# Strassen weight sums: three POOL adds per pair replaced by three more accumulating DMAs

## The chip, the core and the metric

The kernel runs on one core of a Trainium2 chip. The metric is the device time of one execution in microseconds. Engines: PE multiplies matrices, DVE, ACT and POOL work element by element, SP only issues transfers. Each engine takes its instructions in a fixed order and waits at the head of its queue.

## The reference

One inference step of a two-layer decoder: 512 prompt tokens and 64 sample tokens, width 1024, all in fp32.

```
h = RMSNorm(x)
P = h @ w_in                      # projections of four mixers, and gate logits G (4 x 1024 columns)
o_b = mixer_b(P_b)                # HGRN2, GLA, RWKV-7, RetNet, 256 wide each
x = x + (sum_b sigmoid(G_b) * (o_b @ w_branch[b])) @ w_out
g, u = split(RMSNorm(x) @ w_ffn_in)          # 2 x 2816 columns
x = x + (silu(g) * u) @ w_ffn_out
```

After the last layer `y = RMSNorm(x)`. The outputs are y for both groups and the mixers' states.

## The kernel before

Activations lie with channels on the partitions and the 576 tokens in the free dimension, in two halves of 288. An fp32 product is made of three fp16 matmuls: a value is split into a high part (ACT: scaled copy to fp16, L1692) and a low part (DVE: the value times 256 less the high part, L1693); then high x high, high x low and low x high are added in PSUM (L1718 to L1720).

Two places use Strassen's scheme in Winograd's form: the last two gate groups of each layer (`last_gates`, 8 pairs per layer) and most of the first feed-forward product (`ffn`, 19 pairs per layer, one for each 128 columns of g and of u). A pair takes two blocks of 128 output columns and the whole input depth of 1024, cut in two: four fp32 blocks of weights a11, a12, a21, a22, each 128 partitions x 512. Seven products (12 matmuls each) instead of eight use the blocks A11, A12, A22 and four sums of blocks: S1 = A21 + A22, S2 = S1 - A11, S3 = A11 - A21, S4 = A12 - S2. The sums of tokens (T4, tiles `st` and `mt`) are made once per layer.

`strassen_weights` makes the weights of one pair, as a generator in nine steps. In step 2 POOL issues a DMA that adds a22 to a21 where it lies (L1698). In steps 3 to 5 A11, A22 and A12 are split, and after each split POOL overwrites the block with a difference (L1696). In steps 6 to 9 the four sums are split. `strassen` makes the seven products of a pair; after each product it advances the generators: steps 6 to 9 of the present pair after products 1 to 4, steps 2 to 5 of the next pair after products 4 to 7. DVE then adds up products (su and sc, L1734). In the feed-forward stage sc goes through Silu on ACT (fsg, L1763), a product on DVE (fy, L1765) and a split (fa, L250); in the gates through Tanh, a product with the branch (gu, L1539) and an add on POOL (mg, L1540).

The written order is not the last word: a scheduler with its own costs sets the order of instructions on each engine. Weights are loaded by SP's queue into rings of a few buffers; the accumulating DMAs are on POOL's queue, where each waits for its operands before it is issued.

Of the kernel before, what the change touches and what calls it, by code (L numbers as in the profile page):

```python
# [16 lines left out]
ADD, SUB, MUL, MAX, MIN = ALU.add, ALU.subtract, ALU.mult, ALU.max, ALU.min  # L17
# [157 lines left out]
class Net:  # L175
# [14 lines left out]
    def t(self, ring, shape, name, dt=F32):  # L190

        assert int(np.prod(shape[1:])) * (2 if dt == F16 else 4) <= SIZE[ring], (shape, name)
        return self.rings[ring].tile(list(shape), dt, tag=ring, name=name)
# [51 lines left out]
    def split(self, out_hi, out_lo, src, scale=1.0):  # L245

        nc = self.nc
        nc.scalar.activation(out_hi, src, AF.Copy, scale=scale)
        if scale == 1.0:
            nc.vector.tensor_tensor(out_lo, src, out_hi, op=SUB)  # L250
        else:
            nc.vector.scalar_tensor_tensor(out_lo, src, scale, out_hi, op0=MUL, op1=SUB)
# [1410 lines left out]

    def strassen_tokens(self):

        nc = self.nc
        out = [self.t("gd", [128, 4, 2, HW], f"st{i}", F16) for i in range(4)]
        h0, h1 = slice(0, HW), slice(HW, T)  # L1670
        src = []
        for k in range(4):
            b11, b12, b21, b22 = (self.x[k + o][:, h] for o in (0, 4) for h in (h0, h1))
            for i, (dst, a, b) in enumerate(((b11, b12, b11), (b12, b22, b12), (b22, b22, b11), (b21, b21, b22))):
                nc.gpsimd.tensor_tensor(dst, a, b, op=SUB)
                src.append(((0, 2, 1, 3)[i], k, dst))
        yield out
        for i in (3, 1, 0, 2):
            for j, k, dst in src:
                if i == j:  # L1680
                    self.split(out[i][:, k, 0], out[i][:, k, 1], dst)
            yield out

    def strassen_weights(self, key, load, ring, **rings):

        nc = self.nc
        a11, a12, a21, a22 = load()
        w = self.sw[key] = {}

        def split(name, a):  # L1690
            hl = w[name] = self.t(rings.get(name, ring), [128, 2, 4, 128], "h" + name, F16)
            nc.scalar.activation(hl[:, 0], a, AF.Copy, scale=WS)  # L1692
            nc.vector.scalar_tensor_tensor(hl[:, 1], a, WS, hl[:, 0], op0=MUL, op1=SUB)  # L1693

        def add(dst, a, b, op):
            nc.gpsimd.tensor_tensor(dst, a, b, op=op)  # L1696
        yield
        nc.gpsimd.dma_start(out=a21, in_=a22, accum_op=ADD)  # L1698
        yield
        for name, a, op0, op1 in (("A11", a11, a21, a11), ("A22", a22, a22, a11), ("A12", a12, a12, a11)):  # L1700
            split(name, a)
            add(a, op0, op1, SUB)
            yield
        for name, a in (("S2", a11), ("S1", a21), ("S3", a22), ("S4", a12)):
            split(name, a)
            yield

    def strassen(self, w, t, prep, ps3, ring, then=None):


        nc = self.nc
        h0, h1 = slice(0, HW), slice(HW, T)

        def product(ring, a, rhs):
            ps = self.psum(ring, [128, HW], "fs" + a)
            for k in range(4):
                hi, lo = rhs(k)
                nc.tensor.matmul(ps, w[a][:, 0, k], hi, start=k == 0, stop=False)  # L1718
                nc.tensor.matmul(ps, w[a][:, 0, k], lo, start=False, stop=False)  # L1719
                nc.tensor.matmul(ps, w[a][:, 1, k], hi, start=False, stop=k == 3)  # L1720
                if k % 2:
                    yield
            next(prep, None)
            return ps

        def b(o, hs):
            return lambda k: (self.h[k + o][:, 0, hs], self.h[k + o][:, 1, hs])

        def tt(i):
            return lambda k: t(i, k)  # L1730

        def plus(a, p, name):
            o = self.t(ring if name[1] == "c" else "gt", [128, HW], name)
            nc.vector.tensor_tensor(o, a, p, op=ADD)  # L1734
            if then and name[1] == "c":
                then(o)
            return o
        p1 = self.t("gt", [128, HW], "sp1")
        nc.scalar.copy(p1, (yield from product("b", "A11", b(0, h0))))
        c11 = plus(p1, (yield from product("b", "A12", b(4, h0))), "sc11")  # L1740
        p4 = yield from product("g", "A22", tt(3))
        u2 = plus(p1, (yield from product("b", "S2", tt(1))), "su2")
        p5 = yield from product("g", "S1", tt(0))
        u4 = plus(u2, p5, "su4")
        u3 = plus(u2, (yield from product(ps3, "S3", tt(2))), "su3")
        c22 = plus(u3, p5, "sc22")
        c21 = plus(u3, p4, "sc21")
        c12 = plus(u4, (yield from product(ps3, "S4", b(4, h1))), "sc12")
        return c11, c12, c21, c22

    def ffn(self, l):
# [191 lines left out]
```

## Time and profile before

| | us |
|---|---|
| median of three runs (lowest, highest) | 2241.27 (2237.95, 2241.97) |
| the profiled execution | 2235.82 |
| its span in the trace | 2234.1 |
| PE busy in the span | 2047.3 (92%) |
| DVE busy | 1677.4 (75%) |
| ACT busy | 1070.6 (48%) |
| POOL busy | 652.0 (29%) |

An engine's share is a mean over stages with different limits: the feed-forward stage alone (784 to 988 us in layer 0) looks different. A busy matmul of 0.29 us overlaps the next ones. The first feed-forward product lies at 735 to 988 us (its first three column blocks without Strassen), the last gates at 530 to 690.

### The profile page before, as it was taken

Reading aid. Unit: us, or ns where it says so; the run is one execution under the profiler, and the core shown is the slowest. Engines: PE = TensorE matmul, PEld = TensorE weight load, DVE = VectorE, ACT = ScalarE, POOL = GpSimd, SP = SyncE. Lnnn points to the kernel's source line nnn. Section 1 sums busy time; section 2 is a strip of 40 time slices with the busy share of each in tenths; the row PEclk is TensorE's granted clock in tenths of the full one; section 3 lists DMA queues with packets and bytes.
Section 4 is the critical chain, followed back from the end, with each engine's and each line's share of the span. In section 5 each row is a group of like instructions: output and inputs, shape, how many; then the busy total and the mean of one; then the engine's idle time right before and its main releaser. Section 6 shows DMA issues by size and latency. Waiting matters only on the chain.

```text
span 2234.1 us, 42266 instructions
## 1 busy us (share of the span) xinstructions
PE 2047.3 (92%) x15754; PEld 1616.7 (72%) x15754; DVE 1677.4 (75%) x3719; ACT 1070.6 (48%) x2400; POOL 652.0 (29%) x850
## 2 busy tenths in 40 slices
PE   7988899898989999999998889889998988999998
PEld 5766676686767677777776667768776766777776
DVE  7889856868786899973488996686687768998531
ACT  6554545436454655442466344363554455554332
POOL 2212212245550544320011131222365415443000
PEclk9999999999999999999999999999999999999999
DMA  6312213333436244343421222142344443443431
GB/s 179 82 36 66 54 52 91 94 77 84 108 100 200 59 118 126 88 132 108 120 69 51 54 56 60 51 116 72 79 98 104 124 144 93 118 116 93 126 105 50
DMA packets 373497, 209.58 MB, mean 94 GB/s; under 512 B 59810, under 2 KB 360410, under 8 KB 373292
## 3 DMA queue, kind: packets, MB, share of 16 engines
q1 hardware_dynamic: 365516, 192.73, 31.1%
q0 software_dynamic: 7776, 14.16, 3.5%
q8 instruction: 124, 2.03, 0.4%
q14 instruction: 81, 0.66, 0.1%
HBM read 173.72 MB, written 16.59 MB: 85 GB/s over the span
## 4 chain that ended last, share of the span: by engine, by line
PE 47%; DVE 31%; ACT 8%; issue 7%; DMA 4%; POOL 3%; SPq 0%; DVEq 0%; ACTq 0%; POOLq 0%
PE pb L243 4%; PE pb L241 4%; PE pb L242 4%; PE xb L243 4%; PE xb L242 4%; PE xb L241 4%; DVE hA L1693 3%; DVE hS L1693 2%; DVE whl L229 2%; DVE sc L1734 2%; DVE fy L1765 2%; DVE qg L1111 2%; PE fsS L1720 2%; PE fsS L1718 2%; PE fsS L1719 2%
## 5 line engine op out<-in xcount | busy, mean ns | idle before, releaser
L241 PE MATMUL pb<-h,whl 128*128 128x288 f16 (+1 forms) x1504 | 439.9, 293 | 3.7 <-ACT h L463 2.2
L243 PE MATMUL pb<-h,whl 128*128 128x288 f16 (+1 forms) x1504 | 439.7, 293 | 2.7 <-DVE whl L229 2.7
L242 PE MATMUL pb<-h,whl 128*128 128x288 f16 (+1 forms) x1504 | 439.5, 292 | 0.6 <-DVE h L464 0.4
L229 DVE SCALAR_TENSOR_TENSOR whl<-raw,whl 128x512 f16<-128x512 f32 (+1 forms) x352 | 251.7, 725 | 132.0 <-ACT whl L228 130.3
L243 PEld LDWEIGHTS <-whl 128*128 128x128 f16 (+1 forms) x2784 | 277.3, 100 | 88.4 <-issue 11.0
L242 PEld LDWEIGHTS <-whl 128*128 128x128 f16 (+1 forms) x2784 | 276.7, 99 | 87.4 <-issue 11.0
L241 PEld LDWEIGHTS <-whl 128*128 128x128 f16 (+1 forms) x2784 | 279.0, 100 | 77.0 <-issue 3.6
L228 ACT ACTIVATE whl<-raw 128x512 f16<-128x512 f32 (+1 forms) x352 | 213.0, 616 | 167.4 <-PE pb L243 58.1
L243 PE MATMUL xb<-fa,whl 128*128 128x288 f16 x704 | 201.3, 286 | 0.0
L242 PE MATMUL xb<-fa,whl 128*128 128x288 f16 x704 | 201.3, 286 | 0.0
L241 PE MATMUL xb<-fa,whl 128*128 128x288 f16 x704 | 201.3, 286 | 0.0
L1718 PE MATMUL fsA<-h,hA 128*128 128x288 f16 x432 | 123.5, 286 | 14.4 <-DVE gu L1539 9.1
L1718 PE MATMUL fsS<-st,hS 128*128 128x288 f16 x456 | 131.1, 287 | 6.0 <-ACT hS L1692 6.0
L1720 PE MATMUL fsS<-st,hS 128*128 128x288 f16 x456 | 131.2, 288 | 0.9 <-DVE hS L1693 0.9
L1719 PE MATMUL fsS<-st,hS 128*128 128x288 f16 x456 | 131.1, 287 | 0.0
L1720 PE MATMUL fsA<-h,hA 128*128 128x288 f16 x432 | 123.6, 286 | 1.6 <-DVE hA L1693 1.6
L1719 PE MATMUL fsA<-h,hA 128*128 128x288 f16 x432 | 123.5, 286 | 0.0
L1696 POOL TENSOR_TENSOR raw<-raw 128x512 f32<-128x512 f32 x52 | 79.5, 1529 | 133.8 <-DVE hA L1693 129.7
L1718 PEld LDWEIGHTS <-hS 128*128 128x128 f16 x864 | 85.1, 99 | 35.5 <-ACT hS L1692 14.1
L1693 DVE SCALAR_TENSOR_TENSOR hA<-sraw,hA 128x512 f16<-128x512 f32 x110 | 101.5, 930 | 10.4 <-ACT hA L1692 9.7
L1696 POOL TENSOR_TENSOR sraw<-sraw 128x512 f32<-128x512 f32 x60 | 89.9, 1501 | 50.0 <-DVE hA L1693 45.5
L1720 PEld LDWEIGHTS <-hS 128*128 128x128 f16 x864 | 85.2, 99 | 24.6 <-DVE hS L1693 3.0
(487 smaller groups left out, 5271.1 us busy)
## 6 DMA issues: line engine op xcount, KB each, us to landing
raw<-in_w_in SPq DMA_DIRECT2D x208, 256.0 KB
sraw<-in_w_ffn_in SPq DMA_DIRECT2D x40, 512.0 KB
raw<-in_w_ffn_out SPq DMA_DIRECT2D x80, 256.0 KB
raw<-in_w_ffn_in SPq DMA_DIRECT2D x78, 256.0 KB
x<-xd SPq DMA_DIRECT2D x32, 288.0 KB
raw<-sraw POOLq DMA_DIRECT2D x34, 256.0 KB, 3.3
sraw<-in_w_in SPq DMA_DIRECT2D x32, 256.0 KB
raw<-in_w_out SPq DMA_DIRECT2D x32, 256.0 KB
```

The costliest lines, as they stand in the source:

```text
L228: nc.scalar.activation(hl[:, 0, :n], raw[:, :n], AF.Copy, scale=WS)
L229: nc.vector.scalar_tensor_tensor(hl[:, 1, :n], raw[:, :n], WS, hl[:, 0, :n], op0=MUL, op1=SUB)
L241: nc.tensor.matmul(ps, wh, hi, start=i == 0, stop=False)
L242: nc.tensor.matmul(ps, wh, lo, start=False, stop=False)
L243: nc.tensor.matmul(ps, wl, hi, start=False, stop=i == len(ks) - 1)
L1111: nc.vector.tensor_tensor(qo, qq, ee, op=MUL)
L1693: nc.vector.scalar_tensor_tensor(hl[:, 1], a, WS, hl[:, 0], op0=MUL, op1=SUB)
L1696: nc.gpsimd.tensor_tensor(dst, a, b, op=op)
L1718: nc.tensor.matmul(ps, w[a][:, 0, k], hi, start=k == 0, stop=False)
L1719: nc.tensor.matmul(ps, w[a][:, 0, k], lo, start=False, stop=False)
L1720: nc.tensor.matmul(ps, w[a][:, 1, k], hi, start=False, stop=k == 3)
L1734: nc.vector.tensor_tensor(o, a, p, op=ADD)
```

## The change

All four sums are made by accumulating DMAs on POOL's queue, which can only add. So the sums get other signs: a11 becomes A11 + A21, a21 becomes A21 + A22, a22 becomes A22 + A11 + A21, a12 becomes A12 + A22 + A11 + A21. This is the scheme for the weights with the first row of blocks negated; DVE puts it right when it adds up the products (`su2` and `c12` subtract). A block is still split as A before the DMA overwrites it. The products S1 and S2 change places.

```
-        def add(dst, a, b, op):
-            nc.gpsimd.tensor_tensor(dst, a, b, op=op)
-        yield
-        nc.gpsimd.dma_start(out=a21, in_=a22, accum_op=ADD)
-        yield
-        for name, a, op0, op1 in (("A11", a11, a21, a11), ("A22", a22, a22, a11), ("A12", a12, a12, a11)):
-            split(name, a)
-            add(a, op0, op1, SUB)
-            yield
-        for name, a in (("S2", a11), ("S1", a21), ("S3", a22), ("S4", a12)):
-            split(name, a)
-            yield
+        def add(dst, a):
+            nc.gpsimd.dma_start(out=dst, in_=a, accum_op=ADD)
+        yield
+        split("A11", a11)
+        add(a11, a21)
+        yield
+        add(a21, a22)
+        split("A22", a22)
+        yield
+        add(a22, a11)
+        split("A12", a12)
+        yield
+        split("S3", a11)
+        yield
+        split("S1", a21)
+        add(a12, a22)
+        yield
+        split("S2", a22)
+        yield
+        yield
+        split("S4", a12)
+        yield
...
-        c11 = plus(p1, (yield from product("b", "A12", b(4, h0))), "sc11")
+        c11 = sum2(p1, ADD, (yield from product("b", "A12", b(4, h0))), "sc11")
         p4 = yield from product("g", "A22", tt(3))
-        u2 = plus(p1, (yield from product("b", "S2", tt(1))), "su2")
         p5 = yield from product("g", "S1", tt(0))
-        u4 = plus(u2, p5, "su4")
-        u3 = plus(u2, (yield from product(ps3, "S3", tt(2))), "su3")
-        c22 = plus(u3, p5, "sc22")
-        c21 = plus(u3, p4, "sc21")
-        c12 = plus(u4, (yield from product(ps3, "S4", b(4, h1))), "sc12")
+        u2 = sum2((yield from product("b", "S2", tt(1))), SUB, p1, "su2")
+        u4 = sum2(u2, ADD, p5, "su4")
+        u3 = sum2(u2, SUB, (yield from product(ps3, "S3", tt(2))), "su3")
+        c22 = sum2(u3, ADD, p5, "sc22")
+        c21 = sum2(u3, ADD, p4, "sc21")
+        c12 = sum2((yield from product(ps3, "S4", b(4, h1))), SUB, u4, "sc12")
```

The order on POOL, in the middle of layer 0's feed-forward stage, over two pairs before (a pair has one DMA and three adds; the DMA of the pair with raw_11102 stands among the adds of the pairs ahead of it):

```order
L1696 TENSOR_TENSOR raw_10796<-raw_10800,raw_10796 128x512
L1696 TENSOR_TENSOR sraw_10802<-sraw_10802,raw_10796 128x512
L1698 DMA sraw_10951<-sraw_10951 128x512
L1696 TENSOR_TENSOR raw_10798<-raw_10798,raw_10796 128x512
L1698 DMA raw_11102<-sraw_11104 128x512
L1696 TENSOR_TENSOR sraw_10949<-sraw_10951,sraw_10949 128x512
L1696 TENSOR_TENSOR sraw_10951<-sraw_10951,sraw_10949 128x512
L1696 TENSOR_TENSOR sraw_10949<-sraw_10949 128x512
```

and of the change, at the stage's end (the last two pairs of a layer, then the next layer's norm):

```order
L1697 DMA raw_12006<-raw_12010 128x512
L1697 DMA raw_12010<-sraw_12012 128x512
L1697 DMA sraw_12012<-raw_12006 128x512
L1697 DMA raw_12008<-sraw_12012 128x512
L1697 DMA sraw_12159<-sraw_12161 128x512
L1697 DMA sraw_12161<-sraw_12161 128x512
L1697 DMA sraw_12161<-sraw_12159 128x512
L1697 DMA sraw_12159<-sraw_12161 128x512
L464 TENSOR_TENSOR h2_13915<-nrm_13934,h2_13915 128x288
```

All four DMAs of a pair now stand together, each writing or reading what the one before wrote or read, and no DMA of a later pair stands among them.

The order on DVE, in the middle of the stage before, around the split of S4 of one pair (hS4_11171) and of A11 of the next (hA11_11190):

```order
L1693 SCALAR_TENSOR_TENSOR hS3_11155<-sraw_10802,hS3_11155 128x512
L1734 TENSOR_TENSOR su3_10911<-su2_10873,fsS3_10894 128x288
L1734 TENSOR_TENSOR sc22_10913<-su3_10911,fsS1_10875 128x288
L1734 TENSOR_TENSOR sc21_10915<-su3_10911,fsA22_10840 128x288
L1693 SCALAR_TENSOR_TENSOR hS4_11171<-raw_10798,hS4_11171 128x512
L1734 TENSOR_TENSOR sc12_10934<-su4_10892,fsS4_10917 128x288
L1765 SCALAR_TENSOR_TENSOR fy_10939<-sc21_10915,fsg_10937 128x288
L1693 SCALAR_TENSOR_TENSOR hA11_11190<-sraw_10949,hA11_11190 128x512
```

and of the change, for the same pair (hA11_11174 is A11 of the next pair, whose a11 is sraw_10951):

```order
L1694 SCALAR_TENSOR_TENSOR hS2_11140<-sraw_10804,hS2_11140 128x512
L1745 TENSOR_TENSOR sc11_11143<-sp1_11108,fsA12_11127 128x288
L1694 SCALAR_TENSOR_TENSOR hS4_11171<-raw_10800,hS4_11171 128x512
L1694 SCALAR_TENSOR_TENSOR hA11_11174<-sraw_10951,hA11_11174 128x512
L1694 SCALAR_TENSOR_TENSOR hA22_11192<-sraw_10953,hA22_11192 128x512
L1694 SCALAR_TENSOR_TENSOR hA12_11213<-sraw_10951,hA12_11213 128x512
L1745 TENSOR_TENSOR su2_11195<-fsS2_11178,sp1_11108 128x288
```

A11 of the next pair stands directly behind S4 of this pair; S2 now stands next to S4, with the one sum sc11 between them. On ACT the high parts stand in the same order.

## Rows read from the trace of the kernel before

**Rows 1.** Chain of waits, 817 to 841 us: start us, us, what.
```profile
by line: DVE fy L1765 24.6%; issue 20.6%; DVE hA L1693 18.5%; DVE sc L1734 13.9%; DVE hS L1693 11.7%; DVE su L1734 9.9%; DVE fa L250 1.5%
...
817.26 1.52 DVE fy L1765
...
828.12 2.11 DVE fy L1765
...
839.58 1.52 DVE fy L1765
```

**Rows 2.** Busy time by stretch: us, then PE, PEld, DVE, ACT, POOL, PEclk, DMA, GB/s.
```profile
0.00:40.00 40.00, 29.47 (x200) 22.18 (x201) 28.24 (x77) 24.72 (x61) 13.65 (x35) 1.00 0.76 223
...
720.00:760.00 40.00, 33.60 (x235) 25.13 (x236) 31.39 (x47) 23.94 (x42) 17.00 (x19) 0.88 0.28 81
...
822.40:844.80 22.40, 21.41 (x176) 16.96 (x174) 22.33 (x37) 11.52 (x24) 10.34 (x9) 1.00 0.46 120
```

**Rows 3.** PE in order of time, last product of the stage: start us, us, instruction.
```profile
985.93 0.29 PE L1718 MATMUL fsS<-st,hS 128*128 128x288 f16 x1
...
987.65 0.29 PE L1720 MATMUL fsS<-h,hS 128*128 128x288 f16 x1
```

**Rows 4.** All engines in order of time, 817 to 821 us.
```profile
817.05 1.42 POOL L1696 TENSOR_TENSOR raw<-raw 128x512 f32<-128x512 f32 x1 [4.74 <-DVE hA L1693]
...
817.26 1.52 DVE L1765 SCALAR_TENSOR_TENSOR fy<-sc,fsg 128x288 f32<-128x288 f32 x1
...
819.53 1.35 POOL L1696 TENSOR_TENSOR sraw<-sraw,raw 128x512 f32<-128x512 f32 x1 [1.06 <-DVE hA L1693]
...
820.04 1.39 DVE L1693 SCALAR_TENSOR_TENSOR hA<-raw,hA 128x512 f16<-128x512 f32 x1
...
820.90 0.88 POOL L1698 DMA_DIRECT2D sraw<-sraw  x1
```

**Rows 5.** Line 1765, whole run: count, duration in ns (min, median, max).
```profile
L1765 DVE SCALAR_TENSOR_TENSOR fy<-sc,fsg x76: 448/452/2112, 793.7 to 2087.4; 128x288 f32<-128x288 f32 x76
```

**Rows 6.** Line 1696, whole run: count, duration in ns (min, median, max).
```profile
L1696 POOL TENSOR_TENSOR sraw<-sraw x60: 1261/1569/1721, 737.4 to 2074.9; 128x512 f32<-128x512 f32 x60
L1696 POOL TENSOR_TENSOR raw<-raw x52: 1261/1570/2250, 537.1 to 2061.0; 128x512 f32<-128x512 f32 x52
L1696 POOL TENSOR_TENSOR sraw<-sraw,raw x50: 1257/1357/1759, 539.0 to 2059.5; 128x512 f32<-128x512 f32 x50
```

**Rows 7.** POOL in order of time, first gate pair of layer 0.
```profile
533.62 1.03 POOL L1698 DMA_DIRECT2D raw<-sraw  x1
...
537.09 1.84 POOL L1696 TENSOR_TENSOR raw<-raw 128x512 f32<-128x512 f32 x1 [1.93 <-DMA raw<-sraw]
```

**Rows 8.** Line 1698: landing of 533.62's DMA, of all, of 776 to 980 us.
```profile
DMA to landing us min/median/max: 3.4/3.4/3.4
...
DMA to landing us min/median/max: 3.2/3.3/5.4
...
DMA to landing us min/median/max: 3.2/3.2/4.4
```

**Rows 9.** DVE, POOL and ACT in order of time, 773 to 778 us.
```profile
773.83 0.68 DVE L1693 SCALAR_TENSOR_TENSOR hA<-raw,hA 128x512 f16<-128x512 f32 x1
774.44 0.68 DVE L1693 SCALAR_TENSOR_TENSOR hA<-sraw,hA 128x512 f16<-128x512 f32 x1
...
774.61 2.25 POOL L1696 TENSOR_TENSOR raw<-raw 128x512 f32<-128x512 f32 x1 [5.62 <-DVE hA L1693]
...
776.89 1.15 ACT L1692 ACTIVATE hS<-raw 128x512 f16<-128x512 f32 x2 [0.32 <-POOL raw L1696]
...
777.55 2.97 DVE L1693 SCALAR_TENSOR_TENSOR hS<-raw,hS 128x512 f16<-128x512 f32 x2 [0.38 <-ACT hS L1692]
```

**Rows 10.** DVE in order of time, gu of the fourth and seventh gate pairs.
```profile
622.96 0.81 DVE L1539 SCALAR_TENSOR_TENSOR gu<-sc,ub 128x288 f32<-128x288 f32 x2
...
670.25 0.44 DVE L1539 SCALAR_TENSOR_TENSOR gu<-sc,ub 128x288 f32<-128x288 f32 x1
```

**Rows 11.** Line 1540, whole run: count, duration in ns (min, median, max).
```profile
L1540 POOL TENSOR_TENSOR mg<-mg,gu x64: 784/946/1313, 560.7 to 1777.8; 128x288 f32<-128x288 f32 x64
```

**Rows 12.** The page's DMA queues: packets, MB, share of 16 engines.
```profile
q0 software_dynamic: 7776, 14.16, 3.5%
```

More of the change, by code (lines that the diff above doesn't have):

```diff
@@ L1730, in tt, with sum2 @@
             return lambda k: t(i, k)
-        def plus(a, p, name):
+        def sum2(a, op, b, name):
             o = self.t(ring if name[1] == "c" else "gt", [128, HW], name)
-            nc.vector.tensor_tensor(o, a, p, op=ADD)
+            nc.vector.tensor_tensor(o, a, b, op=op)
             if then and name[1] == "c":
```

## Prediction

> **What bounds the kernel now.** I read four views. First the chain of waits, over one stretch in the middle of the first feed-forward stage [rows 1]: the reader is to see that it names DVE lines only, beside "issue", and no matmul, and that the activation product fy comes back at 817.26, 828.12 and 839.58 us. That is (839.58 - 817.26) / 2 = 11.16 us per Strassen pair. Then the busy time by stretch [rows 2]: there DVE is busy 22.33 of 22.40 us and PE 21.41. Third, PE in order of time [rows 3]: from 985.93 to 987.65 us lie 14 starts, so matmuls start 0.123 us apart (the 0.29 us of each overlaps the next). A product is 12 matmuls, 1.48 us, a pair 84 matmuls, 10.33 us. So the stage runs 0.83 us per pair above PE, and DVE is what it waits for. Fourth, why DVE is that busy [rows 4, 5]: fy takes 0.45 us as a rule (median), but 1.52 when it starts at 817.26, 0.21 us into a 1.42 us add on POOL, and the split of hA at 820.04 takes 1.39 against 0.68 elsewhere [rows 9], again beside an add (819.53 to 820.88). The add stops DVE. The DMA that POOL issues at 820.90 does not: that hA goes on and ends beneath it.
>
> The Trainium skill says the same of the two engines ("SBUF — State Buffer", section "SBUF: two separate sides"): the pair of ports they share is held by one of them for the whole instruction and the other blocks. The rows of fy agree. By that rule alone the change could only help; what it gives is the rival below.
>
> **What goes.** 162 adds on POOL [rows 6], three for each of 54 pairs, 1.4 to 1.6 us each at the median. In the feed-forward stage they hold up DVE about 2.5 us per pair (1.07 of fy, 0.71 each of two splits). Nothing else there waits for POOL.
>
> **What comes.** 162 more accumulating DMAs; each pair now has four, and they are a chain: a11 += a21, then a21 += a22 (which overwrites what the first read), then a22 += a11 (needs both), then a12 += a22. All stand on POOL's one queue, and each waits at its head for the one before it to land, with everything on POOL behind it. Before, a pair had one such DMA, issued a pair ahead. Call a link the time from the issue of one to the start of what waits for it. The trace shows one such wait on an idle POOL [rows 7]: issue at 533.62, the waiting add at 537.09: 3.47 us. From issue to landing it is 3.2 us at the median of 16 in the stage, up to 4.4 there and 5.4 in the whole run [rows 8].
>
> **Why the chain is on the path.** The order of the changed DVE (and ACT) has the split of A11 of a pair behind the split of S4 of the pair before. S4 waits for that pair's fourth DMA; the first DMA of the next pair waits until A11 is split, since it overwrites a11. So no two pairs' chains overlap, and a pair cannot take less than four links and the way from the last landing to the next issue. That way, from [rows 9]: ACT's start to DVE's start on a split 0.66 (776.89 to 777.55), one split to the next on DVE 0.61 (773.83 to 774.44), the second split 0.68, its end to POOL's start 0.10 (774.51 to 774.61): 2.05 us. With a link of 3.47:
> period = 4 x 3.47 + 2.05 = 15.93 us, against 11.16 now and 10.33 that PE needs.
>
> I take 3.47 because it is the only wait seen whole, and because the chain has a DMA in flight nearly all the time, also during the loads of weights, where the longer landings are; the floor is the median landing with the 0.07 us that the waiter at 537.09 took after its own landing (3.4): 3.27, period 15.13. The ceiling I set at 3.9, about half way from the median to the stage's 4.4: period 17.65.
>
> The Trainium skill ("DMA: Bandwidth & Descriptors", section "Anatomy of one DMA — SWDGE (gpsimd) path") gives about 2.0 us and bytes / 436 GB/s for such a DMA, 2.6 us as an estimate for these 256 KB. No landing here is under 3.2 us, so the trace does not agree; by that page the period would be 4 x 2.67 + 2.05 = 12.7 us, still above 11.16.
>
> **The sum for one feed-forward stage.** The first pair's DMAs stand ahead of the stage, in the second normalization, and hurt little: between 0 and one link; I take 0. The second pair's A11 is split at 773.83 on DVE and POOL can issue at 774.61 [rows 9]; the split of S4 of the first pair now stands ahead of it, 0.61 more: 775.2. Seventeen periods to the nineteenth pair: 775.2 + 17 x 15.93 = 1046.0. Its four links: 1059.9. The split of S4 (0.66 + 0.68) and its product (1.48 and the 0.29 of the last matmul): 1063.0. Today the last matmul of the stage ends at 987.65 + 0.29 = 987.9 [rows 3]. So +75.1 us, and +150.2 in two layers, as the second has the same program. What it costs with a link of 3.27: +60.7 a layer; with 3.9: +106. DVE's 2.5 us, and the 0.83 us above PE, are gone but not gained: DVE and PE now wait for the chain. The moved splits and the changed signs cost nothing: as many sums and splits as before, on a DVE that waits.
>
> **The gates.** In the eight pairs of a layer's last gates the recurrent branch sets the pace of the first four; from the gu of the fourth (622.96 us, two in a row, the second from 623.4) to that of the seventh (670.25) are 46.9 us, 15.6 a pair [rows 10]. The chain needs 15.93, and four adds to mg, 0.95 us each [rows 11], stand on POOL behind the fourth DMA; 0.88 and 3.8 us are less than the 5.5 us of a link and the way, so mostly hidden. Bounds per layer: -13 us (twelve adds in the first four pairs that stop DVE for 1.07 us each, all of it on the path) to +15 (all sixteen adds to mg of the last four pairs on the path). I take +4, nearest to the spacing rows: +8 in two layers.
>
> **Total.** The profiled execution took 2235.82 us; + 150.2 + 8 = 2394.0. It lies 5.45 us below the median of the runs, 2241.27, so in their terms 2399.5; I say 2400.
>
> **Rivals.**
> Faster: the lock is the point. If the chains ran a pair ahead of the splits that use them, POOL's adds would be gone from DVE, and the stage would come down to PE: 0.83 us x 18 spacings x 2 = 30 us, 2211. For it: rows 1, 4, 5. Against: the order of the engines, which ties A11 to the S4 before it. It decides where four links and 2.05 us are under 10.33, a link of 2.07. Chance 0.05.
>
> Shorter links. The queue's share in the page [rows 12] is 3.5% of 2234.1 us over 54 DMAs, 1.45 us of transfer each; if a link were only the 0.88 us of issue [rows 4], that and 0.07, it would be 2.40, the period 11.65, the stage's end 986, and the time that of before, about 2241; the landings of 3.2 us and more speak against it. At the 2.67 of the page of the Trainium skill named above, the same sum gives +17.5 a layer, 2276. Chance 0.04, a quarter of it on no change.
>
> Much slower through PE's clock. PE will be busy 10.33 of 15.93 us, 65%, in bursts with pauses of 2 to 3 us. Now the granted clock is 1.00 in the first 40 us with PE busy 74%, and 0.88 from 720 to 760 us with 84% [rows 2], so the share alone does not tell. At the lower level (1.2 GHz) a pair would need 20.7 us on PE and be the bound: (20.7 - 11.16) x 18 x 2 = +343, 2580. Chance 0.04. A drop for a third of the time would still hide in the 5.6 us that PE waits.
>
> Much slower through collisions: all links at the stage's longest landing, 4.4: period 19.65, +142 a layer, 2525. Chance 0.04. That leaves 0.83 for the forecast.
>
> **Numbers.** The forecast's own range, from links of 3.27 and 3.9 with the bounds of the gates drawn in halfway: 2 x (60.7 - 4) = +113 to 2 x (106 + 4) = +220, so 2354 to 2461. I give 2348 to 2455, as long links in every place are the less likely end. 0.2% is 4.5 us, what a measurement of this kernel can tell from no change. Faster 0.05; same 0.02 (the shortest links, and what a half-hidden chain may leave); slower 0.93.
>
> **What would show it.** In the profile after: fy some 16 us apart in the stage; PE idle before fsS matmuls, waiting for ACT's or DVE's split of hS, about 5.6 us a pair; ACT's split of hS waiting for the DMA on most pairs; on POOL four DMAs 3.3 to 3.6 us apart, then some 5.5 us to the next pair's first; fy at 0.45 us nearly everywhere; the stage from 206 us to about 280. It is wrong if the first DMA of a pair is issued before the pair ahead has landed its fourth, if DMAs follow in under 3 us, or if PE's clock falls for whole pairs.

## The result, and the profile after

| | before | after |
|---|---|---|
| median, us | 2241.44 | 2549.0 (2545.42 to 2555.4) |
| profiled execution; its span | 2235.82; 2234.1 | 2555.4; 2553.6 |
| PE, DVE, POOL busy | 92%, 75%, 29% | 85%, 62%, 22% |

The change makes the kernel slower, 1.1375 times the time of before (95% interval 1.135 to 1.1401). I forecast 2400 us and a range up to 2455: the direction and the mechanism were right, three sizes were too small, all to the same side.

The time is lost before the end of each layer's feed-forward stage. PE's last matmul of layer 0's stage starts at 987.65 before [rows 3] and here at

```profile
L1731 PE MATMUL fsS<-h,hS x58: 286/286/448, 900.1 to 1148.5; 128*128 128x288 f16 x58
```

(count, duration in ns as min/median/max, first and last start in us). That is 160.8 us later; twice that is 321.6, and the profiled executions differ by 319.6. The difference has two parts. The first DMA of the second pair is issued 30.1 us late (804.70, the add in its place at 774.61 [rows 9]), nearly all of it from the gates: their last gu starts 28.8 us late (710.13 against 681.33). The other 130.7 us arise in the stage itself. This is POOL's queue there, in order of time (start us, us, instruction; in brackets how long the engine stood idle before it, and what ended that):

```profile
865.69 0.86 POOL L1697 DMA_DIRECT2D sraw<-sraw  x1 [5.51 <-DVE hA L1694]
869.17 0.86 POOL L1697 DMA_DIRECT2D sraw<-sraw  x1 [2.63 <-DMA sraw<-sraw]
872.93 0.86 POOL L1697 DMA_DIRECT2D sraw<-sraw  x1 [2.90 <-DVE sc L1745]
876.66 0.86 POOL L1697 DMA_DIRECT2D sraw<-sraw  x1 [2.87 <-DVE fa L250]
882.83 0.86 POOL L1697 DMA_DIRECT2D raw<-raw  x1 [5.31 <-DVE hA L1694]
888.81 0.86 POOL L1697 DMA_DIRECT2D raw<-sraw  x1 [5.12 <-DMA raw<-raw]
892.61 0.86 POOL L1697 DMA_DIRECT2D sraw<-raw  x1 [2.94 <-DMA raw<-sraw]
897.02 0.86 POOL L1697 DMA_DIRECT2D raw<-sraw  x1 [3.55 <-DMA sraw<-raw]
903.15 0.86 POOL L1697 DMA_DIRECT2D sraw<-sraw  x1 [5.27 <-DVE hA L1694]
```

Each DMA waits for the one before it to land, and a pair's first one waits for the split hA of its A11, as forecast. But the steps are longer: 3.48, 3.76, 3.73, 6.17 us in the first pair, 5.98, 3.80, 4.41, 6.13 in the second. (At 872.93 and 876.66 the releaser named is a DVE instruction; the steps are as long as where a DMA is named.) Over 17 pairs, from 804.70 to 1131.59, the four steps are 5.00, 4.15, 4.09 and 5.98 us at the mean, a period of 19.23; forecast were 3.47 three times, 5.52, and 15.93.

Who waits is seen on ACT in the same stretch:

```profile
888.61 0.63 ACT L1693 ACTIVATE hS<-raw 128x512 f16<-128x512 f32 x1 [5.84 <-DMA raw<-raw]
892.13 0.63 ACT L1693 ACTIVATE hS<-raw 128x512 f16<-128x512 f32 x1 [2.90 <-DMA raw<-sraw]
...
896.52 0.63 ACT L1693 ACTIVATE hS<-sraw 128x512 f16<-128x512 f32 x1 [1.76 <-DMA sraw<-raw]
...
900.90 0.63 ACT L1693 ACTIVATE hS<-raw 128x512 f16<-128x512 f32 x1 [3.42 <-DMA raw<-sraw]
```

All four splits of sums wait for a landing. Over the whole run, the lines on L1697 of the view by line say the same:

```profile
who waited for it (us, times):
  ACT hS L1693: 518.7, 190
...
DMA to landing us min/median/max: 3.2/3.6/6.9
```

Before, the landing was 3.2, 3.3 and 5.4 at most [rows 8].

That this loop sets the pace is also what the profile's chain of waits says. In this trace it does not reach back to layer 0; in the same stage of layer 1, from 2200 to 2260 us, it is (start us, us, what):

```profile
by line: DMA sraw<-sraw 45.3%; DMA raw<-raw 17.1%; issue 12.3%; DMA raw<-sraw 11.5%; DMA sraw<-raw 6.5%; DVE hA L1694 4.4%; ACT hS L1693 3.2%; DVE sc L1745 1.5%; DVE fy L1776 0.6%; POOLq L1697 0.4%; DVE hS L1694 0.2%; DVEq L1694 0.0%
...
2202.29 3.77 DMA sraw<-sraw
2206.05 0.28 issue
2206.34 3.20 DMA sraw<-sraw
...
2209.56 0.04 POOLq L1697
2209.60 0.49 issue
2210.09 3.18 DMA sraw<-sraw
...
2213.84 3.17 DMA sraw<-sraw
...
2217.03 0.64 ACT hS L1693
...
2218.74 0.61 DVE hA L1694
...
2219.64 4.99 DMA raw<-raw
```

Four landings, the split of S4, the split of A11, and the next pair's first DMA: the DMAs of sums make 80% of the chain, and no PE instruction stands in it, with PE's granted clock at 0.89 there.

The stops of DVE are gone, as forecast: its fy, 2112 ns at most before [rows 5], is now never above 459 (line 1776, the same columns):

```profile
L1776 DVE SCALAR_TENSOR_TENSOR fy<-sc,fsg x76: 445/451/459, 843.7 to 2408.4; 128x288 f32<-128x288 f32 x76
```

The queue of the DMAs has four times the packets of [rows 12], 31104.

PE's granted clock fell in the stage (busy time by stretch, columns as in [rows 2]):

```profile
800.00:840.00 40.00, 25.07 (x182) 18.51 (x181) 16.21 (x33) 12.01 (x26) 6.89 (x8) 0.89 0.53 122
1080.00:1120.00 40.00, 28.65 (x167) 17.68 (x167) 19.86 (x40) 13.87 (x28) 6.88 (x8) 0.79 0.55 121
```

It was 1.00 before [rows 2]; in the nine such stretches of this stage it is 0.79 to 0.96, a mean between its two levels, 2.4 and 1.2 GHz. PE had been waiting for splits between its bursts in these stretches, for 48 us in all of the 348 from 800 to 1148 (44.5 for ACT's, 3.4 for DVE's). Whether the clock costs time is a question for the experiments.

### The profile page after: what moved, and what is told of

The parts are those of the page before. It is cut to its first block, busy times and chain, and to the rows that moved or that the text cites. A ratio compares the mean times of both kernels' runs of the same rounds, so it can differ in the third digit from the quotient of the medians.

```text
span 2553.6 us, 42408 instructions
## 1 busy us (share of the span) xinstructions
PE 2159.9 (85%) x15754; PEld 1647.0 (64%) x15754; DVE 1585.3 (62%) x3719; ACT 1079.0 (42%) x2400; POOL 551.7 (22%) x850
## 5 line engine op out<-in xcount | busy, mean ns | idle before, releaser
L1694 DVE SCALAR_TENSOR_TENSOR hS<-sraw,hS 128x512 f16<-128x512 f32 x130 | 111.4, 857 | 220.0 <-ACT hS L1693 220.0
L1693 ACT ACTIVATE hS<-sraw 128x512 f16<-128x512 f32 x130 | 81.7, 629 | 294.1 <-DMA sraw<-sraw 205.1
L1729 PE MATMUL fsS<-st,hS 128*128 128x288 f16 x456 | 146.9, 322 | 66.3 <-ACT hS L1693 61.9
L1729 PEld LDWEIGHTS <-hS 128*128 128x128 f16 x864 | 91.3, 106 | 139.8 <-ACT hS L1693 113.6
L1694 DVE SCALAR_TENSOR_TENSOR hS<-raw,hS 128x512 f16<-128x512 f32 x86 | 59.9, 696 | 176.2 <-ACT hS L1693 176.1
L1729 PE MATMUL fsA<-h,hA 128*128 128x288 f16 x432 | 133.0, 308 | 34.5 <-DVE gu L1539 21.7
L1730 PEld LDWEIGHTS <-hA 128*128 128x128 f16 x648 | 68.7, 106 | 140.5 <-issue 119.6
L1693 ACT ACTIVATE hS<-raw 128x512 f16<-128x512 f32 x86 | 54.1, 629 | 239.2 <-DMA raw<-sraw 116.8
L1697 POOL DMA_DIRECT2D sraw<-sraw x96 | 82.7, 861 | 323.0 <-DMA sraw<-sraw 162.9
L1731 PE MATMUL fsS<-st,hS 128*128 128x288 f16 x456 | 143.4, 319 | 6.2 <-DVE hS L1694 5.8
L1730 PE MATMUL fsS<-st,hS 128*128 128x288 f16 x456 | 144.4, 319 | 0.0
```

The lines of the kernel that those rows point to most:

```text
L1697: nc.gpsimd.dma_start(out=dst, in_=a, accum_op=ADD)
```

## Experiments

My theory after the result: in the feed-forward stage a pair lasts as long as its chain of four DMAs and the way back to the next pair's first one; the same waits of ACT at the head of its queue cost the gates. Rivals: PE, by its lower clock or a wait of its own, sets the pace; the steps are long by themselves and not through the loads; the gates were as cheap as forecast. "Changed" below means an edit to the kernel after, "before" one to the kernel before. The run of before beside each was at 2240.2 to 2240.5 us.

**What are the gates worth?** Changed, with the old sums and signs in the last gates alone (lines shortened; the two `_b` functions are those of the kernel before):

```
-        prep = [self.strassen_weights(i, ...) for ...]
+        prep = [self.strassen_weights_b(i, ...) for ...]
...
-            c = yield from self.strassen(self.sw[i], ...)
+            c = yield from self.strassen_b(self.sw[i], ...)
```

> The gates' pairs make their weight sums as before (one DMA and three POOL subtractions, S2 before S1), the feed-forward pairs keep the four DMAs. Theory (in the gates ACT's and DVE's splits stand in line waiting for DMAs of the chain, with the recurrent branch's work and the branch products behind them; the last gu of layer 0 came 28.8 us later, 710.1 against 681.3): the gates come back, 2549 - 2 x 28.8 = 2491 us, and the feed-forward stage keeps its period of 19.2 us per pair. Rival (the gates' loss is only the feed-forward's later buffers and transfers reaching back, or the 30 us are lost in the normalization): within 10 us of 2549.

2492.5 us (ratio 1.1123, 1.1091 to 1.1155): the gates are worth 56 us, twice the 28.8 read from the trace, where the forecast had 8 for both layers. The feed-forward stage keeps its period (19.06 us over 17 pairs), and the second pair's first DMA is issued at 776.07 instead of 804.70, so the late start of the stage did come from the gates.

**Is it the loop through A11?** Changed, with the next pair's step ahead of this pair's, so that A11 is split ahead of S4:

```
-                    if q < 4:
-                        next(now)
                     if q > 2 and then:
                         next(then)
+                    if q < 4:
+                        next(now)
```

> Two lines change places in both loops: after the fourth product the next pair's step comes before the present pair's, so that the split of A11 of the next pair stands ahead of the split of S4 on DVE and ACT, and the next pair's first DMA needs no landing of the fourth. The same DMAs, bytes and splits. Theory (a closed chain of four links and the way back through S4 and A11, 19.2 us): the period falls to three links and one issue, by the means in the trace of the change 4.97 + 4.15 + 4.08 + 0.88 = 14.1 us, so 2549 - 2 x 17 x 5.1 = 2375 us from the feed-forward alone, 2340 with some of the gates. Rival (the accumulating DMAs' 57 MB, or POOL's issue of 216 of them, is what costs, wherever A11 stands): period stays at 18 or more, 2520 or more.

2463.7 us (1.0994, 1.0956 to 1.1032): 85 us faster, so the loop is on the path, but the gain is half of what I expected.

That is its POOL queue in order of time:

```profile
904.62 0.86 POOL L1697 DMA_DIRECT2D sraw<-raw  x1 [2.87 <-DMA raw<-sraw]
908.99 0.86 POOL L1697 DMA_DIRECT2D raw<-sraw  x1 [3.51 <-DMA sraw<-raw]
911.17 0.86 POOL L1697 DMA_DIRECT2D sraw<-sraw  x1 [1.32 <-DVE hA L1694]
```

and ACT near the end of this stretch:

```profile
908.55 0.63 ACT L1693 ACTIVATE hS<-sraw 128x512 f16<-128x512 f32 x1 [3.75 <-DMA sraw<-raw]
909.09 0.61 ACT L1693 ACTIVATE hA<-sraw 128x512 f16<-128x512 f32 x1
```

From the fourth DMA (908.99) to the next pair's first are 2.18 us here (3.02 in most of the other kind of pair), not 0.88: A11 now stands behind the split of S2, which waits for the landing of the third DMA, the same event that releases the fourth. So a tie one link shorter is left. I had overlooked it. Over 17 pairs the period is (1078.27 - 800.79) / 17 = 16.32 us, one break of 13.0 us near the stage's end included, whose cause stays open; (19.23 - 16.32) x 17 x 2 = 99 us is near the 85 measured.

**Is it PE's wait for PSUM, or its clock?** Changed, with the product A22 in the ring of PSUM buffers "b" instead of "g":

```
-        p4 = yield from product("g", "A22", tt(3))
+        p4 = yield from product("b", "A22", tt(3))
```

> Only the PSUM ring of product A22 changes (from g with two buffers to b with four). In the trace of the change PE stands up to 7.7 us before A22, waiting for DVE's sc, and its matmuls start 0.24 us apart afterwards (granted clock at its lower level). Theory (the chain of DMAs sets the period and PE's pauses and clock lie beside it): PE's pause moves, the granted clock may change, the time stays within 10 us of 2549. Rival (PE's wait for a PSUM buffer and the slow matmuls after it are on the path): A22 runs early, the period falls by 2 us or more, 2549 - 70 = 2480 or less.

2553.4 us (1.1381, 1.1348 to 1.1413): no change.

The waits of PE before A22's matmuls over the stage, 800 to 1148 us (us in total, times, longest), in the kernel after:

```profile
PE fsA L1729 <- DVE sc L1745: 40.3, 10, 7.7
```

and in this run:

```profile
PE fsA L1729 <- DVE su L1745: 27.0, 7, 5.9
```

The wait at A22 got shorter, PE's other waits grew by as much (96 us in all in both), and nothing came of it; the clock was as low as in the kernel after (0.83 from 1080 to 1120 us). PE's wait at A22 is not on the path.

**Is the chain itself the price?** Before, with S2's sum left on POOL, with the other sign, and the two sums that need it made by DMAs that do not wait for each other (shortened):

```
-        for name, a, op0, op1 in (("A11", a11, a21, a11), ("A22", a22, a22, a11), ("A12", a12, a12, a11)):
+        split("A11", a11)
+        add(a11, a11, a21, SUB)
+        yield
+        for name, a in (("A22", a22), ("A12", a12)):
             split(name, a)
-            add(a, op0, op1, SUB)
+            nc.gpsimd.dma_start(out=a, in_=a11, accum_op=ADD)
             yield
...
-        u2 = plus(p1, ..., "su2")
+        u2 = plus(p1, ..., "su2", SUB)
```

> From the kernel before: a21 += a22 by DMA a pair ahead as there; after the split of A11 one POOL subtraction makes a11 = A11 - S1 = -S2; then two DMAs that do not depend on each other add it: a22 += a11 gives S3, a12 += a11 gives S4; the product of S2 is subtracted in su2. One POOL add per pair instead of three, three DMAs, none of which waits for another's landing on POOL. Theory (a POOL add stops DVE, and DMAs cost nothing where no chain of landings closes): DVE loses two of its three stops, about 1.5 us of 11.16 per pair, and the stage falls to PE's 10.33: 2241 - 0.83 x 18 x 2 = 2211, 2205 to 2225. Rival (the longer wait for two more landings eats it, or accumulating DMAs as such cost): 2241 or more.

2294.2 us (1.0254, 1.0223 to 1.0286): my theory missed. Without the chain five sixths of the loss are gone, but it is no gain.

```profile
840.23 0.63 ACT L1692 ACTIVATE hS<-sraw 128x512 f16<-128x512 f32 x1 [1.94 <-DMA sraw<-raw]
843.41 0.63 ACT L1692 ACTIVATE hS<-raw 128x512 f16<-128x512 f32 x1 [2.55 <-DMA raw<-raw]
```

ACT waits for both landings of a pair, and what stands behind it in its queue waits too. SP's loads of weights wait for landings of sums as well, 135 us in 17 waits from 790 to 985 us, where it has no such wait in the kernel before.

**Are the long steps made by the loads?** Changed, with three sets of blocks loaded per layer and used again in turn:

```
+            if m % 3 in quads:
+                return quads[m % 3]
+            q = quads[m % 3] = []
...
+            for a in q:
+                nc.vector.tensor_scalar(a, a, 1e-4, None, op0=MUL)
```

> The changed kernel; the feed-forward stage loads weights for only three of a layer's pairs and uses those blocks again in turn for the others, scaled down so that they stay in range: it leaves out the other weights, so its output is another. Theory (the links of 4.1 to 6 us are the quiet 3.75 us link lengthened by the weight loads that run in the same DMA engines): four sums a pair as before, 3 x 3.75 + 5.45 = 16.7 us a pair in place of 19.23, that is 2549 - (19.23 - 16.7) x 17 x 2 = 2463 us. Rival (a DMA that waits for a DMA takes that long by itself, loads or not): within 20 us of 2549.

2510.8 us (1.1201, 1.1168 to 1.1235), between the two. POOL in the quiet part of its stage:

```profile
940.30 0.86 POOL L1697 DMA_DIRECT2D raw<-sraw  x1 [4.63 <-DVE hA L1694]
943.82 0.86 POOL L1697 DMA_DIRECT2D sraw<-sraw  x1 [2.65 <-DMA raw<-sraw]
947.57 0.86 POOL L1697 DMA_DIRECT2D sraw<-raw  x1 [2.90 <-DMA sraw<-sraw]
951.32 0.86 POOL L1697 DMA_DIRECT2D sraw<-sraw  x1 [2.88 <-issue]
956.82 0.86 POOL L1697 DMA_DIRECT2D raw<-raw  x1 [4.64 <-DVE hA L1694]
```

3.52, 3.75, 3.75 and 5.50 us: so long are the steps with few loads beside them, the first shorter than the two behind it. Over 17 pairs (818.09 to 1107.53) they are 3.64, 3.83, 3.72 and 5.83, a period of 17.03, near the 16.7 of the theory. The saving, (19.23 - 17.03) x 17 x 2 = 75 us, is halved by the second pair's first DMA, which is issued at 818.09 instead of 804.70 (2 x 13.4 = 27 us): 2549 - 75 + 27 = 2501. So the loads make about 2.2 us of each period. (The run also uses the same three sets of buffers throughout, so the blocks' places were not held fixed.)

**Does a link less shorten the pair?** Changed, without the sum for S4:

```
         split("S1", a21)
-        add(a12, a22)
```

> The changed kernel without the fourth sum of each pair (S4's block is split as it was loaded): it leaves out that part of the computation. Theory (a pair lasts as long as its chain of sums): the chain is three links, and the next pair's first sum waits for the third one's landing and some 2.2 to 3.0 us of splits: 4.97 + 4.15 + 3.75 + 2.2 to 3.0 = 15.1 to 15.9 us a pair in place of 19.23, so 2549 - (19.23 - 15.5) x 17 x 2 = 2422 us or, with what the gates gain, down to 2385. Rival (the stage is paced by something else, the lower clock of the TensorE or the DMA engines' load): above 2500.

2442.0 us (1.0894, 1.0856 to 1.0933), 107 us less. The period is 16.56 (789.78 to 1071.26 over 17): 5.03 and 3.85 for the links, and 7.67 from the third DMA to the next pair's first, where I had expected 6 to 6.8. The chain sets the pace; why the way back without the fourth link is longer than its parts stays open.

**Latency or bytes?** Changed, each DMA adding half its columns:

```
-            nc.gpsimd.dma_start(out=dst, in_=a, accum_op=ADD)
+            nc.gpsimd.dma_start(out=dst[:, :2], in_=a[:, :2], accum_op=ADD)
```

> The changed kernel with each of the four DMAs adding half of its block only (256 of 512 columns): it leaves out the other half of the sums. Theory (a link is mostly the fixed way of a DMA from issue to the word that it has landed): links shorter by under 1 us, a pair 16 to 19 us, 2440 to 2540 us. Rival (a link is mostly the bytes moved): links near half, a pair near 12 us and the time 2310 to 2380 us.

2432.3 us (1.0852, 1.0819 to 1.0884), just under the theory's 2440 and far from the rival. Its period is 16.27 (790.11 to 1066.68 over 17). An undisturbed step on its POOL queue is

```profile
922.46 0.86 POOL L1697 DMA_DIRECT2D raw<-sraw  x1 [4.84 <-DMA raw<-raw]
925.63 0.86 POOL L1697 DMA_DIRECT2D sraw<-raw  x1 [2.31 <-DMA raw<-sraw]
```

and the landings of the whole run

```profile
DMA to landing us min/median/max: 2.6/2.7/5.9
```

3.17 us from 922.46 to 925.63, for 3.75 with whole blocks, and landings of 2.6 us at least for 3.2. Halving the bytes takes off 0.6 us; by these two points 2.0 us of a landing are no matter of bytes (an estimate).

**Can a DMA off the chain replace an add?** Four runs, for a version that beats before. Before, with S4's sum alone made by a DMA (the diff as for two DMAs, with A22's sum an add on POOL):

> The kernel before with one of its three GpSimd sums made by a DMA, that of S4 (S2 is made with the other sign, so that this sum is an addition). Nothing stands behind that DMA in the chain of sums, and its split is the pair's last. Theory (a DMA costs nothing where its landing is not waited for; what costs is the chain): no slower than 2245 us, and up to 20 us faster, if the VectorE's stops behind GpSimd's additions were on the path. Rival (every DMA in place of an addition costs the stage about half of what two cost in the run with two parallel DMAs, by ScalarE's waits): 2267 us.

2259.6 us (1.0079, 1.0055 to 1.0103): slower, nearer to the rival. ACT's split of S4 waits for the landing 3.49 us at 833.52. ACT is not the only one that waits for it: the profile's chain of waits goes on from that landing through a load of weights.

```profile
829.60 3.84 DMA raw<-raw
...
833.98 4.08 DMA raw<-in_w_ffn_in
...
839.16 1.61 POOL sraw L1696
...
842.05 3.62 DMA sraw<-sraw
...
845.75 0.64 ACT hS L1692
...
853.21 3.83 DMA raw<-raw
```

SP's load waits for the landing of S4's sum (64.4 us in 7 times from 790 to 985 us; the kernel before has no such wait there). POOL's DMA for a later pair, issued at 838.60 after 8.12 us of idle, waits for the load, and the adds of the present pair stand behind it in POOL's queue. One round of two pairs takes 23.6 us, 22.3 before [rows 1]. So something did stand behind this DMA.

So the same with that split two steps later, and before with nothing but the later split:

```
-                    if q < 4:
+                    if q in (0, 1, 2, 5):
                         next(now)
```

> The run with S4's sum alone by DMA, with the split of S4 two steps later (ahead of the step in which the next pair's A22 is split, one product ahead of its use). Theory (what that run lost is ScalarE's wait at the split of S4, 3.49 us behind the landing at 833.52, with the VectorE idle behind it, where the kernel before had it 99.7 us busy in 100): without that wait the VectorE has 86.6 us of work in 100 of an 11.5 us pair, that is 9.96 us, and TensorE's 10.33 us a pair set the pace: 2241 - (11.16 - 10.4) x 17 x 2 = 2215 us (2205 to 2235). Rival (the wait only moves: TensorE then waits for a split that comes late): 2255 to 2275.

2249.7 us (1.0049, 1.0034 to 1.0064), between the theory and the rival.

> The kernel before with nothing but the split of S4 two steps later: what the later split does by itself. Theory: nothing waits there, so no change, 2234 to 2248. Rival (a later split costs or gains by itself): more than 10 us off 2241.

2252.8 us (1.0054, 1.0035 to 1.0074), outside my range: the later split alone costs what that run lost, a good part of it in the gates (their last gu in layer 0 starts at 685.6 for 681.3). With the later split in both, the DMA in place of the add makes no difference that these runs can tell. And two parallel DMAs with later splits (`q in (0, 1, 3, 5)`):

> The run with two parallel DMAs, with the split of S3 one step later and that of S4 two steps later. Theory (its 54 us were ScalarE's waits for the landings at these splits): most of them go, 2215 to 2250. Rival (the sums by DMA cost by something else, their traffic or the DMA engines' share of 0.67): 2280 to 2300.

2288.3 us (1.022, 1.0203 to 1.0237), hardly better and within the rival's range. In the stage the later splits did gain: the products with the sums of tokens (`st`) of layer 0 start within 205.0 us, 212.8 without the later splits, 200.0 before. But the gates lose, with the last gu at 697.1 for 690.7.

The busy times from 820 to 900 us (columns as in [rows 2]), first of the kernel before:

```profile
820.00:900.00 80.00, 75.92 (x615) 59.83 (x613) 79.76 (x129) 41.99 (x88) 37.73 (x31) 1.00 0.46 116
```

of before with nothing but the late split:

```profile
820.00:900.00 80.00, 75.43 (x609) 59.34 (x607) 79.32 (x132) 41.18 (x84) 36.80 (x28) 1.00 0.47 121
```

and of one DMA and the late split:

```profile
820.00:900.00 80.00, 75.46 (x614) 59.87 (x613) 70.12 (x133) 41.73 (x86) 30.36 (x29) 1.00 0.59 139
```

One add less takes 10 us in 80 off DVE's busy time (the third of the busy times), and PE gets no more done. ACT still waits for the landing with the late split (2.49 us at 877.29), but that wait is not in the profile's chain there: from 851 to 879 us 29.7% of the chain is a load of weights, which POOL's next DMA waits for with adds behind it. In before with nothing but the late split a load is 21.4% of it (849 to 872 us); in the kernel before none is named [rows 1]. That a block which is split or added to later comes free later for SP's load fits these rows; it was not tried apart. No version beat the kernel before.

## Why the prediction was wrong

Right were the bound before, what goes (DVE's stops), the chain of four on one queue, the loop through A11 behind S4, and that loop as what sets the pace: the queue's rows show it, and the runs without the loop's tie and without a link shorten the pair. The forecast had +79.1 us a layer (75.1 and 4); it is +160.8. What failed is the price of a link, taken from one quiet wait, and the gates, put at almost nothing. The 81.7 us between lie in these steps:

1. **"With a link of 3.47"**, 37 us a layer. I took a term of the quiet chain for all, "also during the loads of weights, where the longer landings are", but 3.47 was measured on one wait, in a gate pair, with one DMA a pair on the queue. With four a pair the steps meet the loads: by the run with few loads 19.23 - 17.03 = 2.20 us a pair, 1.36 of it in the first link (5.00 against 3.64). The rival "collisions" had the right size, 19.65, and I gave it 0.04. My ceiling of 3.9 was half way to a longest landing seen with a quarter of the traffic.
2. **The same term without loads**, 19 us a layer: 17.03 - 15.93 = 1.10 a pair. 3.47 was a landing of 3.4 us and 0.07 to the add. The first link, with a landing of 3.2 and 0.28 to the next issue in the chain above, comes out the same only by luck: 15 of 17 are 3.49 to 3.58 with few loads (mean 3.64). The second and third are 3.75 at rest (means 3.83 and 3.72), as POOL there takes about 0.55 us from the landing to the issue, and the row of before held no such pair. The last step was good as a whole: 3.47 + 2.05 = 5.52 in the forecast, 5.50 at rest and 5.83 at the mean. Its two terms are off against each other, since a landing at rest of 3.2 us leaves 2.3 for the way back.
3. **"The gates ... I take +4"**, 25 us a layer (28.8 less the 4). I let the first four pairs cost nothing, since the recurrent branch set their pace. But ACT and DVE serve that branch too, and their queues stand still at a split that waits for a landing. ACT in that stretch:

```profile
545.85 0.63 ACT L1693 ACTIVATE hS<-sraw 128x512 f16<-128x512 f32 x1 [4.66 <-DMA sraw<-sraw]
...
565.95 0.63 ACT L1693 ACTIVATE hS<-sraw 128x512 f16<-128x512 f32 x1 [3.70 <-DMA sraw<-sraw]
```

   The gu of the fourth pair, from 622.96 [rows 10], comes some 16 us later. The other 13 us come in the last four pairs, which take 20.2 us each from the fourth to the seventh, 15.6 before. From the fifth pair to the eighth the last step of their chains is 8.2 to 9.5 us, where I had 5.5; what lengthens it was not tried. The size is shown by the run with the old gates, 56 us in two layers; that ACT's waits carry it is read from these rows and was not tried apart. POOL's queue, which serves the recurrent branch too, holds work of that branch between the same DMAs; that is a rival which no run separated.
4. **The start of the chain**, under 1 us: 775.2 was forecast against the 774.61 of before, and 804.70 less the gates' 28.8 is 775.9.

The sum, 37 + 19 + 25 + 1, closes on 81.7. "Nothing else there waits for POOL" was not quite so: ACT's splits waited 11.4 us for adds in the stage before (11 times, 790 to 985 us). It plays no part in the sum.

The rival of the clock did not come true in its form. The clock fell to 0.79 to 0.96 in the stage, but the steps of POOL's queue account for the whole period, and the chain in layer 1 names no PE instruction; that the clock costs nothing beside them is argued from these rows, since no run held it up. The rival "faster" fell further than I gave it: even one DMA for one add, with no sum behind it, is no gain. Its sum of 0.83 us a pair assumed that DVE, freed, would run; by the chains of those runs it waits for landings, and for loads of weights that come late.

The Trainium skill's 2.0 us and bytes / 436 GB/s ("DMA: Bandwidth & Descriptors", section "Anatomy of one DMA — SWDGE (gpsimd) path") fits in its first term and not in its second: the shortest landings, 2.6 and 3.2 us for 128 and 256 KB, give 2.0 us and 0.6 us per 128 KB, about 220 GB/s, half the page's rate (an estimate from two sizes).

## What to carry to other kernels

An operation moved from an engine to a DMA becomes a latency, and it costs that latency wherever an instruction at the head of an engine's queue waits for the landing; count these waits, and what else stands in that queue, before counting the engine time saved. Ask also which load waits for that landing to get a place (64.4 us of such waits in the run with S4's sum alone by DMA). A chain of dependent DMAs should be priced with the longest landings that the trace shows beside heavy traffic, not with the median, and a link from DMA to DMA with a row of that very kind. When pieces are tied in a loop through a queue's order, look for the next tie before expecting that cutting the first one gives its full length.

## What the runs showed of the hardware

Within a chain of accumulating DMAs of 256 KB the second and third step, from issue to issue, were 3.7 to 3.8 us wherever nothing disturbed them, in the kernel after and in three experiments. The first step, behind a pause of the queue, was about 3.5. The landings are alike, about 3.2 us; in the chain shown above POOL issues 0.28 us behind the first landing and about 0.55 us behind the next two, with an instruction of its sequencer (POOLq) in between. In the kernel after the first step was 3.48 us at best and 7.22 at worst; beside few loads 16 of 17 stayed under 3.8.

In the kernel after, the third step is 4.4 us in every second pair (nine times of 17 between 4.36 and 4.42) and 3.7 to 3.8 in the others; with few loads it is never above 3.81. In each of the nine SP issues loads of weights 0.9 us after the DMA, and the DMA engines are busy 66 to 68% of the step; in seven of the other eight it is 39 to 41%.
